# Splitting the output weights early and reloading both parts from DRAM

## The chip, the cores and the metric

One Trainium2 chip, one core of it. The metric is the device time of one execution in microseconds (us). Unchanged programs give times that spread by some tenths of a per cent from run to run.

## The reference

One decoder layer over 1024 tokens of width 1024, in float32:

```python
h      = x @ w_in                      # pool part | q | k | v | forget gate
pool   = pool_mixer(...)               # 512 columns, four groups of 128
attn   = forgetting_attention(...)     # 512 columns, 8 heads of 64, causal
x      = layer_norm(ALPHA * x + concat(pool, attn) @ w_out)
x      = layer_norm(ALPHA * x + square(relu(x @ w_mlp1)) @ w_mlp2)
```

The change concerns `w_out` alone, a matrix of 1024 x 1024 (4 MB): 8 blocks of 128 rows.

## The kernel before

Float32 products are made of three matmuls: each operand `a` is split into a high part `hi` (a cast to the type fp32r, on ScalarE) and the remainder `lo = a - hi` (a subtraction, on VectorE), and `hi*hi + hi*lo + lo*hi` is summed (`split` at L70 to L72, `three` at L81).

The stages follow each other in program order: projection of v and the gate, three of the four pool groups, the attention in four pairs of heads (`order`, L434), the product with `w_out` and the first layer norm, the two products of the MLP and the second norm. Attention goes in units `(p, e, m)`: pair p, head e of the pair, block m of 256 query rows; 8 units a pair. In the first three pairs m falls from 3 to 0, in the last pair it rises, so that the early rows of the mixer are done first. The loop at L437 makes the probabilities of one unit (`att_probs`) and then the values of the unit before (`att_values`). Between these pieces `fillstep` puts matmuls of another job into TensorE's queue, so that it has work while it waits for VectorE and ScalarE: in the first three pairs the q and k projection of the next pair (`qk_proj`, 96 matmuls each), in the last pair the last pool group (`last_fill`: `pool_group(0)`, 48 matmuls, then `pool_linear(0)`).

In `att_probs` GpSimd adds the causal mask to a row of gate sums (L342, first three pairs only), VectorE adds that row to the scores and takes the minimum (L355), ScalarE takes the exponential (L357). In `att_values` TensorE transposes the probabilities (L377), ScalarE casts them (L378), VectorE forms the remainder (L379), TensorE multiplies with v (L393), and ScalarE and VectorE take the result out (L398, L399).

The order of the instructions on each engine and in each queue is fixed when the program is built: a list scheduler walks the program with a priority by program order and takes a later instruction early when its engine and its buffers are free. So the loads and splits of the output weights (L480 to L486), which stand behind the attention in the program, were taken into the last pair of heads. Each engine then executes its own list in order, and an instruction that waits holds up all behind it.

Buffers in SBUF come from classes with a fixed count: `S` (3 of them) holds float32 data on its way to a split, `B` (14) holds split weights, x and v, `Q` (10) and `A` (9) the rest. Every load of weights for a projection (`load_w`, L74) takes an `S` and a `B`. The split output weights take four `B`, two blocks of rows in each.

At L484 SyncE issues the load of one block of `w_out` into an `S`; L485 splits it into its place in `B`. The mixer's output goes through DRAM (`mix_dram`): the attention's at L400, that of the last pool group at L282. It is loaded at L759, split, and multiplied with the output weights at L785.

Of the kernel before, what the change touches and what calls it, by code (L numbers as in the profile page):

```python
# [8 lines left out]
F32 = mybir.dt.float32  # L9
# [3 lines left out]
ALU = mybir.AluOpType  # L13

P = 128
S = 1024
D = 1024
NT = S // P
KT = D // P
# [6 lines left out]
CH = 512  # L26
# [10 lines left out]
def trunk(ctx, tc, xT, xn, wuqk, wvf, bf, poolw, pscale, wout, g1, b1, w1, w2, g2, b2, out):  # L37
# [5 lines left out]
    nc = tc.nc  # L43
    sb = ctx.enter_context(tc.tile_pool(name="sb", bufs=1, reuse_waits="tile"))
    ps = ctx.enter_context(tc.tile_pool(name="ps", bufs=1, space=bass.MemoryType.PSUM))
    dr = ctx.enter_context(tc.tile_pool(name="dr", bufs=1, space=bass.MemoryType.DRAM))
# [4 lines left out]
    def slot(tag, shape, dt=F32R):  # L51
        uid[0] += 1
        return sb.tile([P] + list(shape), dt, tag=tag, bufs=NBUF[tag], name=f"{tag}{uid[0]}")
# [16 lines left out]
    def split(hi, lo, src):  # L70
        nc.scalar.copy(hi, src)  # L71
        nc.vector.tensor_tensor(lo, src, hi.bitcast(F32), ALU.subtract)  # L72
# [34 lines left out]
    ncf_dram = dr.tile([NH, S], F32, name="ncf_dram")  # L107
    rin_dram = dr.tile([NH, S], F32, name="rin_dram")
    mix_dram = dr.tile([4, P, 8, 256], F32, name="mix_dram")


    xs = {}
# [125 lines left out]
    def run(gen):  # L238
        for _ in gen:
            pass  # L240
# [29 lines left out]
    def pool_linear(g, slots):  # L270
        st = slot("S", [P], F32)
        nc.sync.dma_start(st, poolw[:, g])
        pw = slot("U", [2, P])
        split(pw[:, 0], pw[:, 1], st)
        dh, dl = pooled[g]
        mx = slot(slots, [S], F32)
        for c in range(NCH):
            cs = slice(c * CH, (c + 1) * CH)
            dst = bank("mm" if g in LATE else None)
            three(dst, (pw[:, 0], pw[:, 1]), (dh[:, cs], dl[:, cs]), True, True)  # L280
            nc.scalar.activation(mx[:, cs], dst, AF.Copy, scale=ps_sb[:, g : g + 1])
        nc.sync.dma_start(mix_dram[:, :, g, :].rearrange("m p t -> p m t"), mx.rearrange("p (m t) -> p m t", m=4))  # L282
# [39 lines left out]
    def gate_row(h):  # L322
        if h not in gate_rows:
            gate_rows[h] = slot("A", [S], F32)
            rsum[h] = small([P, NT], "rsum", bufs=3)
            nc.sync.dma_start(gate_rows[h], ncf_dram[h : h + 1, :].to_broadcast([P, S]))
# [94 lines left out]
    def last_fill():  # L421
        for g in LATE:
            yield from pool_group(g, "mm")
            pool_linear(g, "Q")
# [3 lines left out]
    def fillstep():  # L428
        fill["credit"] += fill["rate"]
        while fill["credit"] >= 1.0:  # L430
            fill["credit"] -= 1.0
            next(fill["gen"], None)

    order = [(p, e, m) for p in range(NPAIR - 1) for e in range(2) for m in (3, 2, 1, 0)]  # L434
    order += [(NPAIR - 1, e, m) for m in range(4) for e in range(2)]
    pend = None
    for n, unit in enumerate(order):  # L437
        p = n // 8
        if n % 8 == 0:
            if p + 1 < NPAIR:  # L440
                gen, pieces, over = qk_proj(p + 1, "mm"), 4 * KT + 1, 28
            else:
                gen, pieces, over = last_fill(), (2 * KT + 2) * len(LATE), 14
            fill.update(gen=gen, credit=0.0, rate=pieces / over)
        prob = att_probs(*unit)
        if n + 1 < len(order):
            gate_row(2 * order[n + 1][0] + order[n + 1][1])
        if pend is None:
            for g in EARLY[1:]:
                pool_linear(g, "A")  # L450
        fillstep()
        if pend is not None:
            att_values(*pend)
        pend = (*unit, prob)
        if n % 8 == 7:
            run(gen)
    att_values(*pend)
# [22 lines left out]
    for kp in range(KT // 2):  # L480
        hi, lo = slot("B", [2, D]), slot("B", [2, D])
        for k in range(2):
            st = slot("S", [D], F32)
            nc.sync.dma_start(st, wout[2 * kp + k])  # L484
            split(hi[:, k], lo[:, k], st)  # L485
            wo.append((hi[:, k], lo[:, k]))  # L486

    def load_row(tag, src):
# [266 lines left out]
    for m in range(4):  # L755
        mh = []
        for half in range(2):
# [8 lines left out]
            hi, lo = slot("Q", [4, 256]), slot("Q", [4, 256])  # L766
# [389 lines left out]
```

## Time and profile before

| | us |
|---|---|
| median of 3 runs | 1048.75 |
| lowest, highest | 1047.0, 1049.51 |
| the profiled execution | 1046.21 |
| its span, first to last instruction | 1044.4 |
| TensorE busy (PE) | 1017.5 |
| VectorE busy (DVE) | 760.6 |
| ScalarE busy (ACT) | 510.3 |
| GpSimd busy (POOL) | 139.0 |

The profile is of one execution, and all durations below are from it. In its views PE is a matmul, PEld the weight load that runs beside it, SPq the queue in which SyncE issues DMAs. A busy time of PE counts a matmul from its start to a modelled end: two of 512 columns in a row start 0.23 us apart and are counted with 0.39 us each, so short gaps between matmuls are not seen as idle time. Stages by the trace: the work ahead of the attention to about 112 us, the first three pairs to about 266 us, the last pair to about 318 us (its last matmuls run among the first ones of the output product), the output product and the first norm to about 344 us, then the MLP.

### The profile page before, as it was taken

What the parts mean: (1) busy time and instruction counts of PE and PEld (TensorE: products, weight loads), DVE (VectorE), ACT (ScalarE), POOL (GpSimd) and SP (SyncE); (2) the same over time, 40 slices, a digit from 0 to 9 for tenths busy, and PEclk for the clock granted to TensorE, in tenths of its full rate; (3) what the DMA queues carried; (4) which work ended last, traced back from release to release, by engine and by line L of the source; (5) the groups of instructions that cost most, each with busy time, mean ns of one, the idle gap of its engine ahead of it and who ended that gap; (6) DMA issues with size and microseconds to landing.
All of it is one profiled execution on the core that took longest, in us unless ns stands there. A gap on an engine that the chain in (4) does not pass through costs nothing.

```text
span 1044.4 us, 13990 instructions
## 1 busy us (share of the span) xinstructions
PE 1017.5 (97%) x4958; PEld 845.5 (81%) x4958; DVE 760.6 (73%) x1296; ACT 510.3 (49%) x818; POOL 139.0 (13%) x243
## 2 busy tenths in 40 slices
PE   7999999999989999999999999999999999999995
PEld 7988888878767888888888888888788888888884
DVE  4466678777896896989887878788875666565546
ACT  4414566666774331677666766768621221122152
POOL 0000012121100021112112122120100000000057
PEclk9999999999999999999999999999999999999998
DMA  6211311111346632139756667565999888878753
GB/s 223 82 48 62 121 54 50 36 49 53 104 138 192 202 138 105 62 112 357 293 225 266 238 242 280 212 266 189 343 321 305 283 260 282 274 228 275 234 177 120
DMA packets 111798, 195.81 MB, mean 187 GB/s; under 512 B 9256, under 2 KB 77672, under 8 KB 111728
## 3 DMA queue, kind: packets, MB, share of 16 engines
q1 hardware_dynamic: 95600, 136.71, 39.5%
q0 software_dynamic: 15840, 57.68, 14.1%
q8 instruction: 39, 0.64, 0.3%
q10 hardware_dynamic: 288, 0.52, 0.1%
q14 instruction: 31, 0.25, 0.1%
HBM read 127.18 MB, written 67.70 MB: 187 GB/s over the span
## 4 chain that ended last, share of the span: by engine, by line
PE 53%; DVE 3%; DMA 2%; issue 1%; POOL 0%; ACT 0%; POOLq 0%; SPq 0%; DVEq 0%; ACTq 0%
PE s L962 15%; PE s L608 10%; PE pv L962 8%; PE pt L608 7%; PE mm L608 6%; PE pv L608 4%; PE pt L962 2%; PE mm L962 2%; DVE B L72 1%; DMA S<-in_w_dram 1%; DMA A<-hid_dram 1%; DMA hid_dram<-A 0%; POOL A L562 0%; DVE A L731 0%; ACT A L730 0%
## 5 line engine op out<-in xcount | busy, mean ns | idle before, releaser
L71 ACT CAST B<-S 128x1024 fp32r<-128x1024 f32 (+1 forms) x92 | 78.5, 870 | 171.4 <-DMA S<-in_w_dram 58.6
L72 DVE TENSOR_TENSOR B<-S,B 128x1024 fp32r<-128x1024 f32 (+1 forms) x92 | 90.3, 995 | 33.5 <-ACT B L71 33.5
L608 PE MATMUL s<-B,Q 128*128 128x512 f32 x480 | 113.5, 390 | 0.1
L608 PEld LDWEIGHTS s<-B,Q 128*128 128x128 f32 x480 | 90.0, 188 | 19.2 <-ACT B L71 0.5
L962 PE MATMUL s<-B,Q 128*128 128x512 f32 x390 | 94.8, 390 | 0.0
L962 PEld LDWEIGHTS s<-B,Q 128*128 128x128 f32 x390 | 73.2, 188 | 15.5
L71 ACT CAST Q<-S 128x1024 fp32r<-128x1024 f32 x52 | 54.5, 1050 | 60.4 <-PE s L608 17.0
L962 PE MATMUL s<-B,A 128*128 128x512 f32 x333 | 83.1, 394 | 0.9 <-DMA A<-hid_dram 0.9
L733 POOL DMA_DIRECT2D hid_dram<-A x90 | 48.4, 542 | 219.0 <-ACT A L730 174.2
L962 PEld LDWEIGHTS s<-B,A 128*128 128x128 f32 x333 | 62.5, 188 | 15.5 <-DMA A<-hid_dram 1.4
L72 DVE TENSOR_TENSOR Q<-S,Q 128x1024 fp32r<-128x1024 f32 x52 | 63.3, 1218 | 12.1 <-ACT Q L71 12.0
L608 PE MATMUL pt<-B,Q 128*128 128x512 f32 x300 | 71.6, 389 | 0.0
L608 PE MATMUL mm<-B,Q 128*128 128x512 f32 x300 | 71.6, 389 | 0.0
L393 PE MATMUL pv<-A,B 128*128 128x256 f32 x320 | 63.0, 298 | 4.9 <-ACT A L378 2.8
L393 PEld LDWEIGHTS pv<-A,B 128*128 128x128 f32 x320 | 50.4, 190 | 20.2 <-ACT A L378 10.1
L608 PEld LDWEIGHTS pt<-B,Q 128*128 128x128 f32 x300 | 56.3, 188 | 11.7
L608 PEld LDWEIGHTS mm<-B,Q 128*128 128x128 f32 x300 | 56.3, 188 | 11.7
L379 DVE TENSOR_TENSOR A<-pt,A 128x512 fp32r<-128x512 f32 (+1 forms) x80 | 49.0, 634 | 15.7 <-ACT A L378 15.2
L357 ACT ACTIVATE A<-A,nm 128x1024 f32<-128x1024 f32 (+7 forms) x64 | 49.6, 776 | 18.7 <-DVE nm L355 17.5
L731 DVE TENSOR_TENSOR A<-A,A 128x1024 f32<-128x1024 f32 x45 | 53.6, 1220 | 0.5 <-ACT A L730 0.4
L342 POOL TENSOR_TENSOR A<-A,maskb 128x128 f32<-128x128 f32 x48 | 22.4, 467 | 235.9 <-DVE nm L355 136.6
L962 PE MATMUL pv<-B,Q 128*128 128x512 f32 x204 | 50.3, 390 | 0.0
(408 smaller groups left out, 2305.6 us busy)
## 6 DMA issues: line engine op xcount, KB each, us to landing
hid_dram<-A POOLq DMA_DIRECT2D x105, 512.0 KB, 3.9
S<-in_w_dram SPq DMA_DIRECT2D x62, 512.0 KB, 3.5
Q<-hid_dram SPq DMA_DIRECT2D x101, 256.0 KB, 4.6
A<-hid_dram SPq DMA_DIRECT2D x79, 256.0 KB, 5.1
S<-in_wuqk_dram SPq DMA_DIRECT2D x12, 512.0 KB, 3.2
A<-ncf_dram SPq DMA_DIRECT2D x8, 512.0 KB, 3.6
S<-in_wout_dram SPq DMA_DIRECT2D x8, 512.0 KB
S<-mix_dram SPq DMA_DIRECT2D x8, 512.0 KB, 5.1
```

The lines of the kernel that those rows point to most:

```text
L71: nc.scalar.copy(hi, src)
L72: nc.vector.tensor_tensor(lo, src, hi.bitcast(F32), ALU.subtract)
L342: nc.gpsimd.tensor_tensor(nb[:, qs], nb[:, qs], maskb, ALU.add)
L357: nc.scalar.activation(pt[:, :nk], pt[:, :nk], AF.Exp, bias=nm, scale=-1.0, accum_out=rsum[h][:, i : i + 1])
L379: nc.vector.tensor_tensor(tt[:, 1, ev], tp[:, ev], tt[:, 0, ev].bitcast(F32), ALU.subtract)
L393: nc.tensor.matmul(ov, V[j][:, h].rearrange("p s d -> p (s d)"), tt[:, s, a:b], start=(j == 0 and s == 0), stop=(j == 2 * m + 1 and s == 1),)
L608: nc.tensor.matmul(dst, b[x][:, k], A[a][y][:, k], start=first and k == 0 and i == 0, stop=k == H - 1 and i == 2, skip_group_check=not first,)
L731: nc.vector.tensor_tensor(x, x, hi.bitcast(F32), ALU.subtract)
L733: nc.gpsimd.dma_start(hid_dram[self.u, :, i, AT[name] : AT[name] + 2 * CH], part.rearrange("p q n t -> p (q n t)"))
L962: nc.tensor.matmul(dst, h[:, p_], w[q_], start=first and u == self.us[0] and j == 0, stop=u == self.us[-1] and j == 2, skip_group_check=no ...
```

## The change

Each block of `w_out` is loaded, cast and subtracted within the first three pairs of heads, after the values of the units numbered 2, 4, 6, 10, 12, 14, 18 and 20; both parts lie in an `S` buffer, and GpSimd writes them to a new DRAM tensor, 512 KB each. The subtraction is made in two halves of 512 columns. Where the split stood before, SyncE now issues two loads for each block, of the high part and of the remainder, straight into their place in `B`; the cast and the subtraction there are gone.

```diff
+    wo_dram = dr.tile([KT, 2, P, D], F32, name="wo_dram")
...
+    def split_output_weights(k):
+
+        st, hi = slot("S", [D], F32), slot("S", [D])
+        nc.sync.dma_start(st, wout[k])
+        nc.scalar.copy(hi, st)
+        for c in (slice(0, CH), slice(CH, D)):
+            nc.vector.tensor_tensor(st[:, c], st[:, c], hi[:, c].bitcast(F32), ALU.subtract)
+        for i, part in enumerate((hi.bitcast(F32), st)):
+            nc.gpsimd.dma_start(wo_dram[k, i], part)
+
+    SPLIT_AT = {2: 0, 4: 1, 6: 2, 10: 3, 12: 4, 14: 5, 18: 6, 20: 7}
...
         pend = (*unit, prob)
+        if n in SPLIT_AT:
+            split_output_weights(SPLIT_AT[n])
...
         for k in range(2):
-            st = slot("S", [D], F32)
-            nc.sync.dma_start(st, wout[2 * kp + k])
-            split(hi[:, k], lo[:, k], st)
+            for i, part in enumerate((hi, lo)):
+                nc.sync.dma_start(part[:, k].bitcast(F32), wo_dram[2 * kp + k, i])
             wo.append((hi[:, k], lo[:, k]))
```

## Rows read from the trace of the kernel before

**Rows 1.** The page: busy time of each engine, and the shares of the chain that ended last.

```profile
PE 1017.5 (97%) x4958; PEld 845.5 (81%) x4958; DVE 760.6 (73%) x1296; ACT 510.3 (49%) x818; POOL 139.0 (13%) x243
...
PE 53%; DVE 3%; DMA 2%; issue 1%; POOL 0%; ACT 0%; POOLq 0%; SPq 0%; DVEq 0%; ACTq 0%
```

**Rows 2.** Busy time of each engine by stage: the stretch and its length, then PE, PEld, DVE, ACT and POOL with the number of instructions, the granted clock of TensorE as a share of full speed, the busy share of the DMA engines, GB/s.

```profile
112.00:266.00 154.00, 151.43 (x875) 125.06 (x873) 114.88 (x276) 97.48 (x209) 26.81 (x68) 1.00 0.16 51
...
266.00:298.00 32.00, 31.62 (x190) 25.76 (x189) 26.59 (x73) 24.35 (x59) 2.55 (x8) 1.00 0.38 130
298.00:318.00 20.00, 15.16 (x87) 11.99 (x87) 17.56 (x37) 15.21 (x29) 0.62 (x2) 0.91 0.49 160
...
318.00:344.00 26.00, 25.91 (x135) 21.77 (x134) 17.30 (x28) 10.32 (x17) 0.31 (x1) 1.00 0.56 172
```

**Rows 3.** The same view in pieces of 2 us at the end of the last pair.

```profile
300.00:302.00 2.00, 1.43 (x13) 1.14 (x12) 1.91 (x4) 2.00 (x5) 0.00 (x0) 1.00 0.01 4
302.00:304.00 2.00, 1.03 (x10) 0.79 (x8) 2.00 (x4) 1.62 (x3) 0.31 (x1) 1.00 0.00 1
304.00:306.00 2.00, 1.27 (x5) 0.77 (x5) 2.00 (x5) 0.81 (x2) 0.00 (x0) 1.00 0.13 33
306.00:308.00 2.00, 1.53 (x4) 1.24 (x5) 2.00 (x6) 0.36 (x1) 0.00 (x0) 0.66 0.70 244
308.00:310.00 2.00, 2.00 (x7) 1.71 (x7) 1.97 (x4) 1.90 (x4) 0.00 (x0) 0.50 0.09 27
310.00:312.00 2.00, 1.60 (x10) 1.17 (x10) 0.92 (x3) 2.00 (x6) 0.00 (x0) 0.98 1.03 295
...
314.00:316.00 2.00, 0.70 (x7) 0.47 (x6) 1.48 (x7) 1.97 (x5) 0.14 (x1) 1.00 0.67 228
```

**Rows 4.** TensorE's instructions in order of time, 296 to 326 us: start, duration, line, output and inputs, count, and in brackets how long the engine had been idle and what ended that. The last row is the first matmul of the output product.

```profile
301.41 0.51 PE L393 MATMUL pv<-A,B 128*128 128x256 f32 x2 [0.57 <-ACT A L378]
...
304.28 0.73 PE L83 MATMUL mm<-Q,U 128*128 128x512 f32 x2 [1.25 <-ACT Q L71]
...
306.46 0.65 PE L84 MATMUL mm<-Q,U 128*128 128x512 f32 x1 [0.92 <-DVE Q L72]
...
315.88 0.51 PE L393 MATMUL pv<-A,B 128*128 128x256 f32 x2 [1.30 <-ACT A L378]
...
318.44 0.50 PE L83 MATMUL s<-B,Q 128*128 128x512 f32 x1
```

**Rows 5.** VectorE in the same stretch. `B<-S,B` is the subtraction of an output weight block, `Q<-Q,Q` at L72 that of the last pool group.

```profile
297.54 1.22 DVE L72 TENSOR_TENSOR B<-S,B 128x1024 fp32r<-128x1024 f32 x1
...
304.08 1.20 DVE L72 TENSOR_TENSOR B<-S,B 128x1024 fp32r<-128x1024 f32 x1
305.20 1.21 DVE L72 TENSOR_TENSOR Q<-Q,Q 128x1024 fp32r<-128x1024 f32 x1
...
308.75 1.22 DVE L72 TENSOR_TENSOR B<-S,B 128x1024 fp32r<-128x1024 f32 x1
```

**Rows 6.** ScalarE from 284 us on. L251 takes out the first half of the last pool group's projection, `B<-S` is the cast of an output weight block, `Q<-Q` that of the last pool group.

```profile
285.20 0.56 ACT L251 COPY Q<-mm 128x512 f32<-128x512 f32 x1
...
299.92 1.06 ACT L71 CAST B<-S 128x1024 fp32r<-128x1024 f32 x1
...
303.18 1.04 ACT L71 CAST Q<-Q 128x1024 fp32r<-128x1024 f32 x1 [0.18 <-DVE Q L264]
```

**Rows 7.** Groups by line and shape from 266 to 318 us: the eight subtractions and the eight casts of the output weights (count, total busy us, mean ns, idle time of the engine just before them).

```profile
L72 DVE TENSOR_TENSOR B<-S,B 128x1024 fp32r<-128x1024 f32 x8 | 9.7, 1211 | 0.0
...
L71 ACT CAST B<-S 128x1024 fp32r<-128x1024 f32 x8 | 8.4, 1046 | 0.7 <-DMA S<-in_wout_dram 0.7
```

**Rows 8.** GpSimd. The mask adds of 110 to 240 us with shortest, median and longest duration, and who waited for them (us, times); one of them and the VectorE instruction that ran beside it; and, from the MLP, the DMAs that GpSimd issues with 512 KB each: duration of one issue, and time to landing.

```profile
L342 POOL TENSOR_TENSOR A<-A,maskb x38: 425/428/1345, 117.2 to 234.0; 128x128 f32<-128x128 f32 x38
...
  DVE A L355: 2.9, 6
...
175.68 1.34 POOL L342 TENSOR_TENSOR A<-A,maskb 128x128 f32<-128x128 f32 x1 [0.18 <-DVE nm L355]
...
175.52 1.22 DVE L72 TENSOR_TENSOR B<-S,B 128x1024 fp32r<-128x1024 f32 x1
...
L733 POOL DMA_DIRECT2D hid_dram<-A x90: 531/531/767, 464.6 to 739.5; - x90
...
DMA to landing us min/median/max: 2.9/4.0/8.0
```

**Rows 9.** Loads and stores of SyncE's queue: the loads of projection weights (KB, us to landing), one of them and the cast that uses it, the eight loads of output weights (duration of an issue, first and last start), the store of the last pool group's output and the first load of the mixer's output behind it, and how long mask adds had waited for gate rows (us, times).

```profile
S<-in_wuqk_dram SPq DMA_DIRECT2D x3, 512.0 KB, 3.2
...
151.54 0.35 SPq L76 DMA_DIRECT2D S<-in_wuqk_dram  x1
...
167.31 1.03 ACT L71 CAST B<-S 128x1024 fp32r<-128x1024 f32 x1
...
L484 SPq DMA_DIRECT2D S<-in_wout_dram x8: 332/342/348, 224.6 to 297.2; - x8
...
309.15 0.38 SPq L282 DMA_DIRECT2D mix_dram<-Q  x1
...
312.37 0.33 SPq L759 DMA_DIRECT2D S<-mix_dram  x1
...
  DMA A<-ncf_dram: 2.7, 4
```

## The prediction

> **What bounds the kernel now.** I read the page first. TensorE is busy for 97% of the span, and more than half of the chain that ended last is its matmuls [rows 1]. The change adds and removes no matmul, so all it can move is time in which TensorE stands idle or runs slowly. The second view is therefore the busy time by stage [rows 2]: what the reader is to see is the difference between the length of a stretch and PE in it. The first three pairs lose 154.00 - 151.43 = 2.57 us. The last pair loses 0.38 us up to 298 us, and then 20.00 - 15.16 = 4.84 us in its last 20 us, where the granted clock also averages 0.91. The next 26 us lose 0.09. So there is one bad place, and the change takes work out of it.
>
> The third view is that place in pieces of 2 us [rows 3]. VectorE is busy for 1.91 to 2.00 of each 2 us from 300 to 310, while TensorE falls to 1.03. [...] Time lost by the clock: 0.34 x 2 + 0.50 x 2 + 0.02 x 2 = 1.72 us. What the engine did before it fell is in the rows above: it stood idle for 0.57 + 0.97 + 0.73 us in the 6 us ahead. The fourth view, the three engines in order of time, says why [rows 4 to 6]. There is no fill left. TensorE waits 1.25 us for the cast of the last pool group, 0.92 us for its remainder, 0.57 us and later 1.30 us for the cast of transposed probabilities. Among these stand the last casts and subtractions of output weights.
>
> **What the change removes.** Eight subtractions, 9.7 us of VectorE, and eight casts, 8.4 us of ScalarE, all between 266 and 318 us [rows 7]. What each is worth depends on its place:
>
> - The subtraction at 304.08 stands straight ahead of the pool group's remainder at 305.20 [rows 5]. Its input was ready at 303.18 + 1.04 = 304.22 [rows 6], so the remainder can come 1.0 us earlier, and the wait of 0.92 us goes. Value 0.92.
> - The cast at 299.92 delays the next cast, and so TensorE by 0.57 us. But TensorE then reaches the pool group's cast the earlier and waits longer there: 1.25 becomes about 1.8. I count nothing.
> - The wait of 1.25 us is the latency of the pool group's own chain, and that of 1.30 us has only attention work ahead of it. They stay.
> - The clock. With 0.92 us of the idle time gone, the fall may not come. In 314 to 316 us TensorE is busy for only 0.70, and the clock stays up [rows 3]. I take it that the fall goes: 1.72 us.
> - The six splits up to 298 us stand in a stretch that loses 0.38 us in all. I count 0.38 us, as the most they can be worth.
>
> Sum 0.92 + 1.72 + 0.38 = 3.0 us. Lower end 0.9, if the clock falls all the same. Upper end everything but the two waits that stay: 0.38 + 4.84 + 1.72 - 1.25 - 1.30 = 4.4 us.
>
> **What it adds to the first three pairs.** Eight casts of 1.05 us (8.4 us), sixteen half subtractions of 1.21 / 2 = 0.61 us (9.7 us), sixteen GpSimd DMA issues of 0.53 us (8.5 us) [rows 7, 8]. Over the 154 us VectorE goes from 74.6% busy to (114.88 + 9.7) / 154 = 80.9%, ScalarE from 63.3 to 68.8%, GpSimd from 17 to 23% [rows 2]. None becomes the bound. But the engines work in order, so each insertion makes what is behind it later: behind a half subtraction stand the minima of L355 and the remainders of L379, and TensorE waits for both; behind a cast stand L378 and the exponentials. The cover is the fill matmuls and the unit's lead.
>
> How much comes through, from both sides. Lower end: the stretch 266 to 298 us took six splits in 32 us, had fill matmuls as the first pairs have, and lost 0.38 us, so 0.06 us for one, 0.5 us for eight. Upper end: without fill, one cast and one subtraction cost 0.57 and 0.92 us, 0.75 us for each on average, 6.0 us for eight if a split pays that once. The first pairs are nearest to the former: they have fill, and VectorE is 83% busy in those 32 us against 81% here. Because short gaps are not seen in PE's busy time I double the lower end: 0.13 us for each, 1.0 us.
>
> **What moves in the queues.** SyncE's eight loads of output weights move from 225 to 297 us to about 115 to 250 us, past the gate rows, the projection loads and the stores. The DMA engines are 16% busy there, so bandwidth costs nothing. A gate row could come later by the length of a load ahead of it; mask adds already waited for gate rows four times, 2.7 us in all [rows 9]. I take nothing and keep this for the upper end.
>
> The buffers: a split holds two of the three `S`, the longest from its load to the landing of its writes: 3.2 + 1.05 + 1.21 + 2 x 0.53 + 4.0 = 10.5 us [rows 7 to 9]. A projection load needs one. The one shown was issued 15.8 us ahead of its cast and takes 3.2, so it has 12.6 us to spare, more than 10.5. Cost nothing; if two splits come before one load, the cast is up to 21.0 - 12.6 = 8.4 us late, and the fill behind it with it.
>
> In the last pair sixteen loads take the place of eight, and they need `B` directly. Three of the four `B` come free when the first half of the last pool group's projection is done, near 285 us [rows 6]; twelve loads of 0.52 MB are 6.3 MB, at the 295 GB/s of the busiest piece 21 us, so they end near 306 us, ahead of the first use at 318.44. The store at 309.15 and the load at 312.37 stand behind them in the same queue, which makes this the nearest thing to a new wait. Cost nothing; if the loads slip, up to 2 us.
>
> [...] The mask add is between two minima of VectorE: it waits for one and the next waits for it. Its median is 0.43 us, but the one at 175.68 took 1.34 us, and beside it VectorE ran a subtraction of two SBUF inputs from 175.52 to 176.74. So a subtraction stretched a mask add by 0.9 us [rows 8]. [...]
>
> **The sum.** -3.0 + 1.0 = -2.0 us. The profiled execution's 1046.2 us becomes 1044.2. The median of the runs is 2.5 us above the profiled execution, and I shift it by the same amount: 1048.75 - 2.0 = 1046.7 us.
>
> **The rivals.**
>
> 1. *The gain moves on.* The wait that goes is replaced by the next one: TensorE meets the pool group's cast earlier, the clock falls as before, and the first output matmul goes on waiting for store, load and split of the pool group's output (309.15, 312.37, 318.44). For it: two of the four waits are not made by output weights. Against it: the store itself stands behind the removed subtraction. -0.9 + 1.0, about 1048.8 us.
> 2. *GpSimd's queue makes the minima late.* A mask add can stand behind the issue of a write that itself waits for the subtraction, 0.53 us, and be stretched by a half subtraction, 0.61 us. VectorE's next minimum, and with it TensorE, is then up to 1.1 us late for each split. For it: the 1.34 us row; VectorE has waited for mask adds six times already. Against it: those six cost 2.9 us together, and VectorE is idle for 39 us in the stretch. It decides from 3.0 / 8 = 0.38 us for a split: above that the kernel is slower. At 0.8 us: -3.0 + 6.4 = +3.4, 1052.1 us.
> 3. *The whole place closes up.* Without 3.6 us of subtractions VectorE isn't full after 297 us, and all but the two fixed waits go: -4.4 + 0.5 = -3.9, 1044.8 us.
> 4. *It doesn't do what it says:* the scheduler places the loads into `B` so late that the output product waits for them. At 2 us lost this too is about 1048.7 us, and I put it with the first.
>
> **How the numbers follow.** About 0.3%, 3.1 us, is what a measurement of this kernel can tell from no change. Forecast 0.40, first and fourth rival 0.26, second 0.15, third 0.19. Faster by more than 3.1 us means below 1045.6: most of the third and a part of the forecast's own spread (1045.0 to 1048.2), 0.30 together. Slower, above 1051.9: most of the second, 0.14. The rest 0.56. The range leaves out the far ends of the second and third: 1043.5 to 1051.3 us. The likeliest case's own range is 1045.0 to 1048.2.
>
> **What would show it.** Right: in the pieces from 300 to 312 us VectorE below 2.00, the granted clock at 1.00, the wait of 0.92 us gone and the first output matmul 1 to 3 us earlier; in the first three pairs PE's idle time at 3 to 4 us instead of 2.57. The second rival would show as mask adds above 0.43 us and a larger wait of L355 for L342. The first would show as the same waits ahead of the first output matmul, with other names. I am wrong if the scheduler orders the last pool group's chain otherwise, because then the waits that I kept change too.

## The result: the first pairs cost more than the last pair gains

| | before | after |
|---|---|---|
| median, lowest to highest of 20 runs each, us | 1046.38 (1043.6 to 1049.51) | 1050.85 (1047.66 to 1055.65) |
| ratio, 95% interval | | 1.0049 [1.0039, 1.0059] |
| the profiled execution, its span | 1046.21, 1044.4 | 1051.09, 1049.3 |

The change is slower by half a per cent, about 5 us, where 2 us less were forecast. The busy times of TensorE, VectorE and ScalarE hardly differ from [rows 1], as they had to; GpSimd's grow by its writes:

```profile
PE 1018.0 (97%) x4958; PEld 844.7 (81%) x4958; DVE 760.6 (72%) x1304; ACT 510.2 (49%) x818; POOL 149.4 (14%) x259
```

The view that tells is again the busy time by stage (columns as in [rows 2]). In this execution the first pairs begin 3 us sooner than in before and end about 6 us later. The first pairs, then the last pair and the output product:

```profile
112.00:266.00 154.00, 145.79 (x828) 120.33 (x827) 117.28 (x278) 100.80 (x208) 34.38 (x79) 0.98 0.35 119
266.00:298.00 32.00, 30.80 (x181) 23.97 (x180) 22.02 (x64) 17.68 (x49) 3.58 (x10) 1.00 0.51 163
298.00:318.00 20.00, 18.21 (x116) 14.91 (x114) 16.89 (x43) 14.30 (x33) 0.62 (x2) 1.00 0.86 296
318.00:344.00 26.00, 23.81 (x129) 19.34 (x128) 16.59 (x28) 11.12 (x20) 0.62 (x2) 1.00 0.70 212
```

TensorE now loses 154.00 - 145.79 = 8.2 us in the first 154 us, where [rows 2] lost 2.57, and the clock slipped there to 0.98. In pieces of 25 us nearly all of it lies in the first pair. Four pieces of the change, then the first two of before:

```profile
110.00:136.00 26.00, 23.11 (x122) 19.18 (x121) 17.74 (x40) 16.97 (x31) 5.74 (x12) 0.93 0.58 204
136.00:161.00 25.00, 20.60 (x107) 16.68 (x106) 16.22 (x39) 13.31 (x27) 6.30 (x13) 0.93 0.42 144
161.00:186.00 25.00, 24.94 (x144) 20.01 (x144) 22.37 (x55) 17.85 (x38) 6.58 (x14) 1.00 0.47 150
186.00:211.00 25.00, 25.00 (x147) 20.60 (x146) 19.76 (x48) 17.59 (x40) 6.60 (x17) 1.00 0.39 137
...
110.00:136.00 26.00, 25.96 (x141) 21.13 (x140) 18.20 (x43) 15.32 (x30) 3.14 (x8) 1.00 0.22 75
136.00:161.00 25.00, 24.78 (x148) 20.80 (x147) 18.91 (x47) 16.19 (x36) 4.43 (x12) 1.00 0.14 44
```

The first two pieces lose 2.9 + 4.4 us (0.3 in before), the next two 0.1. The splits are not spread as the program places them: the scheduler took them early, so that the eight casts start between 101.97 and 207.03 us, five of them by 157 us, and three fall into the two pieces that lose nothing. The two places in order of time; the first has its cause on ScalarE (SPq is SyncE's issue, x2 two issues with the time between them; L441 loads a block, L442 casts it, L446 writes it out). The last row is from the list of what SyncE's queue waited for (total us, times, longest):

```profile
103.34 0.77 POOL L446 DMA_DIRECT2D wo_dram<-S  x1 [7.17 <-ACT S L442]
...
104.86 0.54 POOL L446 DMA_DIRECT2D wo_dram<-S  x1 [0.75 <-DVE S L444]
...
108.97 12.04 SPq L441 DMA_DIRECT2D S<-in_wout_dram  x2
...
112.56 1.05 ACT L442 CAST S<-S 128x1024 fp32r<-128x1024 f32 x1 [5.28 <-DMA S<-in_wout_dram]
113.63 0.59 ACT L316 ACTIVATE Q<-pt 64x512 fp32r<-64x512 f32 x1
...
116.62 0.45 PE L351 MATMUL s<-Q,Q 128*128 128x384 f32 x1 [2.89 <-DVE nm L357]
...
SPq L441 <- DMA wo_dram<-S: 6.7, 2, 5.1
```

The scheduler put the cast of the second block into ScalarE's list in the first unit, well ahead of its place in the program. It stands there 5.28 us for its load. The load was issued at 108.97, because SyncE waited 5.1 us for the first block's writes to leave their `S` buffer. Behind the cast wait the casts of q (L316), the scores and the minima. So TensorE stands idle (it is busy for 1.73 of the 4 us from 112 to 116), and from 116 to 120 us its clock is down to 0.73. The second place is 30 us later (L402 stores a unit's output, L328 requests the gate row of the next head; the first two rows are the first score matmul and the same request in before, all others are the change's):

```profile
113.57 0.39 PE L349 MATMUL s<-Q,Q 128*128 128x512 f32 x1
...
134.23 0.33 SPq L326 DMA_DIRECT2D A<-ncf_dram  x1
...
110.58 0.39 PE L351 MATMUL s<-Q,Q 128*128 128x512 f32 x1
...
139.90 0.47 SPq L402 DMA_DIRECT2D mix_dram<-U  x1
...
140.42 0.58 SPq L328 DMA_DIRECT2D A<-ncf_dram  x1
...
147.59 0.42 POOL L344 TENSOR_TENSOR A<-A,maskb 128x128 f32<-128x128 f32 x1 [6.85 <-DMA A<-ncf_dram]
147.65 0.69 DVE L357 CUSTOM_DVE_ANT_0 A<-s,A 128x512 f32<-128x512 f32 x1 [3.48 <-DMA A<-ncf_dram]
148.40 0.60 PE L351 MATMUL s<-Q,Q 128*128 128x384 f32 x1 [3.39 <-DVE nm L357]
```

and the stretch around it in pieces of 4 us:

```profile
144.00:148.00 4.00, 1.01 (x6) 0.60 (x5) 0.52 (x2) 1.64 (x3) 0.41 (x2) 1.00 0.92 307
148.00:152.00 4.00, 3.60 (x11) 2.91 (x12) 3.78 (x11) 1.50 (x3) 1.12 (x4) 0.57 0.09 34
```

The gate row's request stands behind a store in SyncE's queue and goes out 29.8 us after the first score matmul, against 20.6 in before; units 0 to 3 come out 5 to 7 us behind before, which is most of these 9 us. The mask add that waits for it starts 7.2 us later (147.59), while the DMA engines are 92% busy with writes of split parts and loads of weights, and TensorE is busy for 1.01 of 4 us. Then the clock falls to 0.57. The row is one line of gate sums for a head, but laid into all 128 partitions it moves as much as the load of a weight block; in before it took 3.6 us to landing:

```profile
A<-ncf_dram SPq DMA_DIRECT2D x8, 512.0 KB, 3.6
...
S<-in_wuqk_dram SPq DMA_DIRECT2D x12, 512.0 KB, 7.4
```

The second row, from the page of the change, shows the same for the loads of projection weights: 7.4 us to landing, 3.2 in before [rows 9].

In the last pair, TensorE in order of time (as [rows 4]; the last row is the first matmul of the output product):

```profile
309.08 0.66 PE L379 MATMUL pt<-ident,A 128*128 128x128 f32 x4 [0.33 <-ACT row L414]
311.65 0.47 PE L351 MATMUL s<-Q,Q 128*128 128x512 f32 x1 [1.21 <-DVE nm L357]
316.91 0.51 PE L395 MATMUL pv<-A,B 128*128 128x256 f32 x2 [0.24 <-ACT A L380]
319.28 0.66 PE L379 MATMUL pt<-ident,A 128*128 128x128 f32 x4 [0.70 <-DVE A L381]
320.67 0.50 PE L395 MATMUL pv<-A,B 128*128 128x256 f32 x2 [0.20 <-ACT A L380]
321.40 0.51 PE L395 MATMUL pv<-A,B 128*128 128x256 f32 x2 [0.22 <-DVE A L381]
325.54 0.50 PE L83 MATMUL s<-B,Q 128*128 128x512 f32 x1 [1.00 <-ACT Q L71]
```

The waits of 1.25, 0.92 and 1.30 us are gone, and so is the fall of the clock. New are 1.21 for minima and 1.00 for the first output product.

### The profile page after: what moved, and what is told of

It reads as the page before. It is cut to its first block, busy times and chain, and to the rows that moved or that the text cites. A ratio compares the mean times of both kernels' runs of the same rounds, so it can differ in the third digit from the quotient of the medians.

```text
span 1049.3 us, 14086 instructions
## 1 busy us (share of the span) xinstructions
PE 1018.0 (97%) x4958; PEld 844.7 (81%) x4958; DVE 760.6 (72%) x1304; ACT 510.2 (49%) x818; POOL 149.4 (14%) x259
## 4 chain that ended last, share of the span: by engine, by line
PE 53%; DMA 2%; DVE 2%; POOL 1%; ACT 0%; issue 0%; POOLq 0%; DVEq 0%; SPq 0%; ACTq 0%
PE s L976 16%; PE s L622 9%; PE pv L976 8%; PE pt L622 6%; PE mm L622 6%; PE pv L622 4%; PE pt L976 2%; PE mm L976 2%; DMA S<-in_w_dram 1%; DMA hid_dram<-A 1%; DMA A<-hid_dram 1%; DVE A L745 0%; DVE B L72 0%; DVE Q L72 0%; POOL A L576 0%
## 5 line engine op out<-in xcount | busy, mean ns | idle before, releaser
L71 ACT CAST B<-S 128x1024 fp32r<-128x1024 f32 (+1 forms) x84 | 70.2, 853 | 171.7 <-DMA S<-in_w_dram 60.5
L72 DVE TENSOR_TENSOR B<-S,B 128x1024 fp32r<-128x1024 f32 (+1 forms) x84 | 80.7, 973 | 35.7 <-ACT B L71 35.7
L622 PEld LDWEIGHTS s<-B,Q 128*128 128x128 f32 x480 | 90.0, 188 | 19.2 <-ACT B L71 0.6
L976 PEld LDWEIGHTS s<-B,Q 128*128 128x128 f32 x390 | 73.2, 188 | 15.6
L71 ACT CAST Q<-S 128x1024 fp32r<-128x1024 f32 x52 | 54.6, 1051 | 62.2 <-PE s L622 17.2
L747 POOL DMA_DIRECT2D hid_dram<-A x90 | 48.2, 539 | 218.6 <-ACT A L744 174.1
L72 DVE TENSOR_TENSOR Q<-S,Q 128x1024 fp32r<-128x1024 f32 x52 | 63.3, 1216 | 14.4 <-ACT Q L71 14.2
L381 DVE TENSOR_TENSOR A<-pt,A 128x512 fp32r<-128x512 f32 (+1 forms) x80 | 49.2, 633 | 16.2 <-ACT A L380 15.7
```

The lines of the kernel that those rows point to most:

```text
L381: nc.vector.tensor_tensor(tt[:, 1, ev], tp[:, ev], tt[:, 0, ev].bitcast(F32), ALU.subtract)
L622: nc.tensor.matmul(dst, b[x][:, k], A[a][y][:, k], start=first and k == 0 and i == 0, stop=k == H - 1 and i == 2, skip_group_check=not first,)
L747: nc.gpsimd.dma_start(hid_dram[self.u, :, i, AT[name] : AT[name] + 2 * CH], part.rearrange("p q n t -> p (q n t)"))
L976: nc.tensor.matmul(dst, h[:, p_], w[q_], start=first and u == self.us[0] and j == 0, stop=u == self.us[-1] and j == 2, skip_group_check=no ...
```

## Markers for all kernels

Times in us from the first score matmul of the same execution (it lies at 110 to 118 us of the span, differing from execution to execution): the start of VectorE's instruction that takes out the output of units 0, 4 and 23 (L399 in before), then the first MLP matmul, then this less unit 23, which is the last pair with the output product. Each row is one profiled execution, and some lie off the median of their kernel: e2 by 3.3, e3 by 4.4 and e11 by 2.1 us below it, e8 by 4.4 above.

| | unit 0 | unit 4 | unit 23 | MLP | MLP - 23 |
|---|---|---|---|---|---|
| before | 15.5 | 41.0 | 165.3 | 304.0 | 138.7 |
| the change | 20.7 | 54.6 | 174.1 | 311.5 | 137.4 |
| e1_lastpair | 15.6 | 41.1 | 164.6 | 302.5 | 137.9 |
| e2_nowrite | 16.4 | 42.4 | 166.4 | 304.2 | 137.8 |
| e3_firstpairs | 19.2 | 51.3 | 171.7 | 309.3 | 137.6 |
| e4_late | 16.3 | 43.7 | 167.2 | 304.3 | 137.1 |
| e5_xwrites | 23.4 | 49.2 | 173.5 | 312.6 | 139.1 |
| e6_behind | 15.5 | 45.1 | 168.6 | 306.1 | 137.5 |
| e7_half | 17.1 | 42.8 | 167.5 | 304.8 | 137.3 |
| e8_late9 | 16.3 | 43.3 | 167.3 | 308.5 | 141.2 |
| e9_gpsub | 15.5 | 41.1 | 169.9 | 313.9 | 144.0 |
| e10_latebehind | 15.6 | 41.2 | 165.9 | 304.2 | 138.3 |
| e11_behind2 | 15.5 | 46.9 | 175.4 | 312.4 | 137.0 |
| e12_rows | 19.4 | 44.3 | 168.2 | 305.1 | 136.9 |
| e13_behindrows | 15.5 | 41.9 | 164.5 | 301.9 | 137.4 |
| e14_lbrows | 15.5 | 41.1 | 164.0 | 300.9 | 136.9 |
| e15_beforerows | 15.6 | 41.1 | 164.9 | 306.6 | 141.7 |

The change falls 5.2 us behind by unit 0 and 13.6 by unit 4, and is 8.8 behind when the first pairs end (9.6 at unit 22: unit 23's output already comes out within the last pair). At the MLP it is 7.5 behind. The two executions as a whole differ by 4.9 only, because the first score matmul of the change lies 3.0 us sooner (110.6 against 113.6 us); whether the change has a part in that is not shown.

## The experiments

The theory formed from the traces: the cost is not the engines' added work but two waits in the first pair, for a load and for a gate row, and both come from the DMA traffic of the splits and from the buffers that it holds. Its rivals: the work on VectorE and ScalarE itself, GpSimd's queue (the second rival of the prediction), and a cost that lies in the last pair. Each of these kernels was run 6 or 12 times, and each ratio is against runs of before that were taken with it; their medians go from 1045.65 to 1047.14 us, so compare ratios and not the medians of different kernels.

**Each half alone.** The last pair as changed, with `wo_dram` filled from x in the v projection and no early split:

```diff
+    for k in range(KT):
+        for i in range(2):
+            nc.gpsimd.dma_start(wo_dram[k, i], xs[1, k].bitcast(F32).rearrange("p a n -> p (a n)"))
...
-        if n in SPLIT_AT:
-            split_output_weights(SPLIT_AT[n])
```

> The last pair alone: no early splits; sixteen loads of prepared parts straight into B, as in the change, where the eight loads, casts and subtractions stood. To have something to load, the DRAM tensor is filled from the x buffers during the projection of v (so the output weights are not the reference's in this kernel). Both theories of the loss (waits for the split's loads, or the added engine work) put the loss into the first pairs, so this kernel should show the gain alone: 2 to 3 us below the kernel before, about 1044 us. If the gain only moves on (first rival of the prediction): within 1 us of before, and the first output matmul as long after the first score matmul as before, 204.8 us.

This kernel leaves the output weights out and multiplies with x's data in their place. Measured 1047.13, 1.0013 [1.0000, 1.0025]. With the filling ahead of it the first score matmul is late (117.5 us, 113.6 in before), so the whole time is no measure of the last pair. From the first score matmul on it is 1.5 us ahead of before at the MLP, and the first pairs are as before.

Then the opposite, the early splits and writes, and the last pair as before:

```diff
-            for i, part in enumerate((hi, lo)):
-                nc.sync.dma_start(part[:, k].bitcast(F32), wo_dram[2 * kp + k, i])
+            st = slot("S", [D], F32)
+            nc.sync.dma_start(st, wout[2 * kp + k])
+            split(hi[:, k], lo[:, k], st)
```

> The first pairs alone: loads, casts, subtractions and writes as in the change, and the last pair splits the original weights again as before. Both theories: the whole loss without the gain. By the trace of the change the outputs of the units ran 9.7 us behind those of before at the end of the first pairs, so 7 to 10 us above before, about 1055 us; ScalarE waits for a split's load by over 4 us once.

Measured 1055.32, 1.0099 [1.0080, 1.0119]. The whole loss is here, and more: in the last pair the predicted waits stand as they were, 1.25 and 0.93 us for the pool group, then 1.41 and 1.29:

```profile
309.09 0.72 PE L83 MATMUL mm<-Q,U 128*128 128x512 f32 x2 [1.25 <-ACT Q L71]
...
311.28 0.50 PE L84 MATMUL mm<-Q,U 128*128 128x512 f32 x1 [0.93 <-DVE Q L72]
```

So taking the splits out of the last pair does remove these waits.

**The work without the writes.** Last pair as before, eight early loads, casts and subtractions, and no write:

```diff
-        for i, part in enumerate((hi.bitcast(F32), st)):
-            nc.gpsimd.dma_start(wo_dram[k, i], part)
```

> The engine work alone: loads, casts and half subtractions in the first three pairs as in the change, but no write to DRAM, so an S buffer is free again at the subtraction; the last pair splits as before. Wait theory (the load of a split waits until the writes of the split before have landed, and ScalarE stands in its queue until that load has landed): no wait of ScalarE above 2 us for a load in the first pair, and 0 to 3 us above before, about 1048 us. Work theory (28 us of added instructions make everything behind them late): the cost stays, 8 to 10 us above before, about 1055 us.

Measured 1047.32, 1.0017 [1.0006, 1.0028]. With all the added work of VectorE and ScalarE the first pairs end 1.1 us behind before in the profiled execution. The load of the second block goes out 3.6 us sooner, and the cast waits 1.62 instead of 5.28:

```profile
105.33 7.07 SPq L441 DMA_DIRECT2D S<-in_wout_dram  x2
...
109.61 1.05 ACT L442 CAST S<-S 128x1024 fp32r<-128x1024 f32 x1 [1.62 <-DMA S<-in_wout_dram]
```

That left open whether the writes hurt by holding `S` or by their traffic. So the same writes, behind the subtraction, but out of x's buffers; `S` is free once the parts are formed (last pair as before):

```diff
+    power2 = small([P, 1], "power2")
...
-        for i, part in enumerate((hi.bitcast(F32), st)):
-            nc.gpsimd.dma_start(wo_dram[k, i], part)
+        seen = nc.gpsimd.tensor_copy(power2, st[:, 0:1])
+        with tc.issue_after(seen.ins):
+            for i in range(2):
+                nc.gpsimd.dma_start(wo_dram[k, i], xs[1, k].bitcast(F32).rearrange("p a n -> p (a n)"))
```

> As the run of the first pairs alone (9.5 us above before), but GpSimd's sixteen writes take their data from a buffer of x and not from the two S buffers of the split; they stay behind the subtraction in GpSimd's queue, so number, size and about the place of the writes are kept, and the S buffers are free at the subtraction (what is written is not the output weights, and nothing reads it). Buffer theory (the loads wait for the landing of writes that hold S): the cost falls to that of the run without writes, 1 to 3 us above before, 1047 to 1049 us. Traffic theory (the writes' 8 MB in the DMA queues and GpSimd's issue time make gate rows and loads late): the cost stays, 7 to 10 us above before, 1053 to 1056 us.

Measured 1052.12, 1.0061 [1.0042, 1.0079]. My theory of the buffer alone fell here: the load goes out early, and its cast waits 3.77 us all the same. Both writes of the first block are under way beside it (issued from 105.30 us), and from 108 to 112 us the DMA engines are 87% busy, against 19% in the run without writes:

```profile
105.46 9.25 SPq L442 DMA_DIRECT2D S<-in_wout_dram  x2
...
111.81 1.05 ACT L443 CAST S<-S 128x1024 fp32r<-128x1024 f32 x1 [3.77 <-DMA S<-in_wout_dram]
119.20 1.05 ACT L443 CAST S<-S 128x1024 fp32r<-128x1024 f32 x1 [3.01 <-DMA S<-in_wout_dram]
```

**Other places.** The splits after the units 8, 10, 12, 14, 16, 18, 20 and 22:

```diff
-    SPLIT_AT = {2: 0, 4: 1, 6: 2, 10: 3, 12: 4, 14: 5, 18: 6, 20: 7}
+    SPLIT_AT = {8: 0, 10: 1, 12: 2, 14: 3, 16: 4, 18: 5, 20: 6, 22: 7}
```

> The change with its eight splits after units 8, 10, 12, 14, 16, 18, 20, 22, so none belongs to the first pair of heads. The work is the same. Wait theory: the two stalls came where two splits in a row and the projection loads of the first pair wanted the same three buffers; the five splits in the second and third pair cost nothing in the trace of the change, so the time is that of before less the gain: 1043 to 1046 us. Work theory: the same 8 to 10 us are lost, later: 1050 to 1053 us.

Measured 1046.12, 1.0002 [0.9991, 1.0013]; 1.9 us behind at the end of the first pairs, and the gain that was expected on top does not show. Late splits with the last pool group's fill over 9 steps instead of 14 (`over = 9`):

> The change with late splits (after units 8 to 22, equal to before within 0.3 us) and the last pool group's matmuls spread over 9 fill steps instead of 14. If the gain of the last pair is lost because the first output matmul waits for the pool group's chain of store, load and cast, that chain starts some 10 us earlier here and the gain comes out: 1 to 3 us below before, 1043 to 1045 us. If the end of the last pair is bound by the attention's own chain, fill matmuls that are gone too early leave TensorE idle: 0 to 3 us above before.

Measured 1047.00, 1.0016 [1.0004, 1.0027]. A miss: 0.14%, about 1.5 us, above the late splits. In the profiled execution, which lies 4.4 us above the median of its twelve, the last pair takes 141.2 us instead of 137.1, TensorE waits up to 1.61 us, and the clock falls to 0.82 and 0.76 at 328 to 336 us. This fits a fill that is used up too early, but no run tests it further. Sixteen half blocks, each with both parts in one `S`:

```diff
+            w = slot("S", [2, CH])
+            hi, st = w[:, 0], w[:, 1].bitcast(F32)
+            nc.sync.dma_start(st, wout[k][:, c])
+            nc.scalar.copy(hi, st)
+            nc.vector.tensor_tensor(st, st, hi.bitcast(F32), ALU.subtract)
+            nc.gpsimd.dma_start(wo_dram[k].rearrange("i p n -> p i n")[:, :, c], w.bitcast(F32))
```

> The change with sixteen half splits: half a block and its high part share one S buffer, each half block is loaded (256 KB), cast, subtracted and written (512 KB, one DMA) by itself. Same bytes, eight loads more, the same number of writes; a split holds one of three S at a time instead of two. Buffer theory: the load of the next half finds a free S, ScalarE's longest wait for a split's load falls from 5.3 to under 2 us, total 1045 to 1048 us. Traffic theory: as the change, 1050 us or more.

Measured 1046.33, 1.0011 [1.0000, 1.0023], with 2.2 us lost in the first pairs; the longest wait of a cast for its load is 3.9 us, not under 2 as expected.

**The first wait removed.** The change, and each cast stands behind the last exponential of its own unit in ScalarE's list:

```diff
+    exps = []
...
-            nc.scalar.activation(pt[:, :nk], pt[:, :nk], AF.Exp, bias=nm, scale=-1.0, accum_out=rsum[h][:, i : i + 1])
+            exps.append(nc.scalar.activation(pt[:, :nk], pt[:, :nk], AF.Exp, bias=nm, scale=-1.0, accum_out=rsum[h][:, i : i + 1]))
...
-        nc.scalar.copy(hi, st)
+        with tc.issue_after(exps[-1].ins):
+            nc.scalar.copy(hi, st)
```

> The change with one edge more: the cast of each split stands behind the last exponential of its own unit in ScalarE's list, so the scheduler cannot take it into an earlier gap. Loads, writes and buffers are as in the change. Wait theory (ScalarE stands at a cast whose load has not landed, and all behind it is late): the stall ahead of the first unit goes, and units run at most 3 us behind before at the end of the first pairs instead of 8.8; total 1045 to 1047 us. Work theory and traffic theory: nothing changes, 1050 to 1051 us.

Measured 1046.79, 1.0004 [0.9993, 1.0014]. No cast of a split waits for its load any more, and unit 0 is as in before. The edge also moves the splits: the first cast starts at 131.64 us instead of 101.97, so this run does not tell the cast's wait from early traffic. At unit 4 it is 4.1 us behind, and GpSimd waits 5.64 us for the gate row. Next, the edge for blocks 0 and 1 alone (`if k < 2`):

> The change, with the cast of blocks 0 and 1 alone behind the last exponential of their unit; the other six stay where the change has them. If the first pair's two stalls are all of the cost, the same as with the edge for all eight, about 4 us below the change and within 1 us of before. If the later six have a part in it, between the two.

Measured 1053.88, 1.0066 [1.0045, 1.0088], no better than the change: a miss that showed a third form of the same wait. With the later casts free to be placed early, splits hold the `S` buffers, two casts wait 3.4 us for a write to leave one, and the casts of projection weights, which feed the fill, wait for loads issued too late:

```profile
173.17 1.04 ACT L71 CAST B<-S 128x1024 fp32r<-128x1024 f32 x1 [4.29 <-DMA S<-in_wuqk_dram]
...
200.97 1.04 ACT L71 CAST B<-S 128x1024 fp32r<-128x1024 f32 x1 [4.76 <-DMA S<-in_wuqk_dram]
```

**The second wait removed.** The change, and the gate row of the next head requested one unit earlier:

```diff
             gate_row(2 * order[n + 1][0] + order[n + 1][1])
+        if n + 2 < len(order) and p < NPAIR - 1:
+            gate_row(2 * order[n + 2][0] + order[n + 2][1])
```

> The change, with one edit: the gate row of the next head is requested one unit earlier in the first three pairs. The second stall (minima waiting 3.48 and mask adds 6.85 us for a gate row that lands late) should go, the first (a cast that waits 5.28 us for its load) stay. If the gate row decides the second stall, 3 to 5 us below the change, about 1 us above before; if the split's cast decides it and the gate row only follows, 0 to 1.5 us below the change.

Measured 1048.22, 1.0017 [1.0004, 1.0030]. The gate row goes out 18.6 us after the first score matmul, and no minimum waits for it; unit 4 comes from 13.6 to 3.3 us behind. So the two waits are not independent: either repair takes some 10 us of unit 4's lag. The first wait stays, as it should:

```profile
110.55 12.03 SPq L441 DMA_DIRECT2D S<-in_wout_dram  x2
...
114.13 1.05 ACT L442 CAST S<-S 128x1024 fp32r<-128x1024 f32 x1 [5.24 <-DMA S<-in_wout_dram]
```

**Both removed, and the control.** The change with both edits, the edge for all eight:

> The change with both repairs: every cast of the early splits behind the last exponential of its own unit, and the gate row of the next head requested one unit earlier. The edge alone left the first output of unit 4 about 4 us behind the kernel before, with GpSimd waiting 5.6 us for a gate row; early gate rows alone left 3 us behind, with the cast waiting 5.24 us for its load. If these two waits are the cost, the first pairs end at most 1 us behind before, and what is left of the gain shows: 0 to 1.5 us below the kernel before. If something third costs, 2 us or more above it.

Measured 1043.36, 0.9965 [0.9952, 0.9977], faster than both kernels. The first pairs end level with before, with all eight splits and all sixteen writes in them: 0.1 us behind at unit 22, and 0.8 us ahead at unit 23, as in the run with the last pair alone:

```profile
112.00:266.00 154.00, 151.78 (x875) 124.88 (x875) 125.03 (x295) 104.15 (x218) 38.88 (x85) 1.00 0.41 137
266.00:298.00 32.00, 31.89 (x195) 25.86 (x195) 21.49 (x67) 20.36 (x56) 2.56 (x8) 1.00 0.73 245
298.00:318.00 20.00, 16.85 (x104) 13.18 (x103) 16.73 (x38) 14.51 (x29) 0.93 (x3) 1.00 0.67 222
318.00:344.00 26.00, 25.65 (x127) 21.04 (x126) 17.90 (x26) 8.05 (x11) 0.00 (x0) 1.00 0.75 212
```

VectorE and ScalarE are busier there than in the change (125.03 against 117.28 us, 104.15 against 100.80), because none of the splits now lies ahead of the stretch and the units come sooner, and TensorE loses 2.22 us, less than in [rows 2]. The first matmul of the output product waits 0.15 us.

Late splits with the edge, and then with both edits:

> Late splits (after the units 8, 10, ... 22) and, in addition, each cast behind the last exponential of its own unit in ScalarE's list. If the late splits still lose something to a cast that stands early, 0.5 to 1 us below the run of late splits, that is up to 1 us below the kernel before. If late splits cost nothing in the first pairs and what is missing of the gain is the last pair's own, the same as the late splits, 1.0000 to 1.0005 of before.

Measured 1045.28, 0.9990 [0.9976, 1.0004].

> Late splits (after the units 8, 10, ... 22), the edge and the early gate rows together, as the most that this placing can give. Late splits with the edge stand at 0.999 of before with 0.6 us lost in the first pairs. If the gate rows still cost something there, 1 us lower; if the 0.6 us is VectorE's and ScalarE's own added work, the same 0.999.

Measured 1043.58, 0.9972 [0.9960, 0.9983]. With both repairs early and late splits are the same within their intervals. And early gate rows on the kernel before, without the change:

> The kernel before, with one edit: the gate row of the next head is requested one unit earlier in the first three pairs. It is the control for the run in which this edit took 2.6 us off the change. If early gate rows help only beside the change's traffic, the same as before, within 0.5 us. If they help by themselves (mask adds waited 2.7 us for gate rows in before), up to 2 us below before, and then that run's gain is no measure of what the change did to the gate rows.

Measured 1046.0, 0.9990 [0.9978, 1.0001]. So early rows by themselves bring 0.1%, about 1 us (by the interval nothing to 0.2%), and the rest of 0.9965 is the change's with its repairs.

**The relief alone.** The kernel before, with the subtraction of the last pair on GpSimd:

```diff
-            split(hi[:, k], lo[:, k], st)
+            nc.scalar.copy(hi[:, k], st)
+            nc.gpsimd.tensor_tensor(lo[:, k], st, hi[:, k].bitcast(F32), ALU.subtract)
```

> The kernel before, with one edit: in the last pair the remainder of the output weights is formed on GpSimd instead of VectorE. Nothing goes through DRAM and nothing is split early, so this is the relief of VectorE at the end of the last pair by itself, without sixteen loads and without any cost in the first pairs. If the predicted terms hold (0.92 of the wait for the pool group's remainder, 1.72 of the clock), the time is 2 to 3 us below the kernel before. If the gain moves on to the next waits, as it did in the run with the last pair alone (about 1 us), the time is 0 to 1.5 us below. If subtractions of 1024 columns on GpSimd stretch VectorE's instructions or come too late for the output product, 1 to 3 us above.

Measured 1055.7, 1.0083 [1.0064, 1.0102], a miss by far. Two subtractions of 2.4 us on GpSimd, and beside them two casts on VectorE, 2.24 and 3.05 us, that take 0.42 us at the median in before; TensorE waits for the minima behind them, and this is half of the loss (4.6 us at unit 23). The last row is a later place: an instruction of a single column, in the pool group's chain, takes 2.30 us (0.15 in before) beside a GpSimd subtraction that started at 308.16, and behind it the clock falls to 0.50 (312 to 316 us):

```profile
272.94 4.85 POOL L486 TENSOR_TENSOR B<-S,B 128x1024 fp32r<-128x1024 f32 x2 [6.12 <-ACT Q L314]
273.35 2.24 DVE L317 CAST Q<-Q 64x512 fp32r<-64x512 f32 x1
...
275.52 3.05 DVE L318 CAST Q<-Q 64x512 fp32r<-64x512 f32 x1
...
278.96 0.58 PE L349 MATMUL s<-Q,Q 128*128 128x256 f32 x1 [4.74 <-DVE nm L355]
...
308.53 2.30 DVE L263 TENSOR_TENSOR Q<-Q,icnt 128x1 f32<-128x1 f32 x1
```

## Why the prediction was wrong, point by point

**The step that failed** is "What moves in the queues" in the first pairs. Three terms were set to nothing. Bandwidth, because the DMA engines were 16% busy: that is a mean, and where the splits' loads and writes meet, the share is 0.92, and from a gate row's request to the mask add that waits for it 7.2 us pass. The gate rows, "I take nothing and keep this for the upper end": 3.48 us of waiting for VectorE, and with the clock's fall to 0.57 behind it most of the second loss. The `S` buffers, "Cost nothing": I compared the time that a split holds them with the spare time of a projection load, and not with the next split's own load, whose cast the scheduler had taken early; it waited 5.28 us. And I had the loads spread over 115 to 250 us, where the casts came between 102 and 207, five of them by 157. The bound that I gave for projection loads, up to 8.4 us, shows in one experiment as 4.29 and 4.76.

Their size by the measured ratios: the change against the change with both repairs is 1.0049 - 0.9965 = 0.84%, 8.8 us; without the 0.1% that early gate rows may bring by themselves, 7.7 us. By the trace the change is 8.8 us behind at the end of the first pairs. I had 1.0 for all of it. My sign for being right, 3 to 4 us without TensorE work in the first pairs, reads 8.2 us, and the first output matmul comes 10.1 us later after the first score matmul than in before (215.0 against 204.9) and not 1 to 3 sooner; with both repairs it comes 0.85 sooner.

That 1050.85 still lies inside 1043.5 to 1051.3 us is luck: these were counted from 1048.75, the median of three runs, which twenty runs put at 1046.38.

**The added work** of VectorE and ScalarE, at 0.13 us for a split, 1.0 in all, was not too low. Without writes it costs 1.1 us by the trace and 0.17%, 1.8 us, by the measured ratio [1.0006, 1.0028], part of it the wait of 1.62; with both repairs nothing can be seen of it.

**The gain of 3.0 us** is of the right order. The run with both repairs stands 0.9990 - 0.9965 = 0.25%, 2.6 us, below the control (each of the two is known to 0.12%). The change stands 1.0099 - 1.0049 = 0.50%, 5.2 us, below the first pairs alone, which had six runs and the wider interval. By the traces it is less: the last column of the markers has a mean of 139.0 us for the five kernels with the splits as before in the last pair (before, e2, e3, e5, e15) and of 137.4 for the ten without them (e8 with its other fill and e9 left out), 1.6 us; counted from unit 22, so that what unit 23 gains is in it, 144.4 and 142.1, 2.3 us. How much it is stays open, since one execution's last pair differs from another's by more (137.6 to 141.7 among those five). By its terms: the wait of 0.92 us went, as predicted. The waits of 1.25 and 1.30 us, which I had kept ("They stay"), went too, and 1.21, 0.70 and 1.00 took their place. The fall of the clock went, but it is no sure price: of the five with the splits in the last pair it shows in before and in the control (0.82 and 0.75 at 316 to 324 us) and not in the other three.

**The rivals.** The first, the gain moves on, happened in part: the first output matmul waits 1.00 us, and the store of the pool group's output is followed by its load after 4.0 us (315.39 to 319.39; 3.2 in [rows 9]), with the DMA engines 0.73 to 1.02 busy in the pieces of 4 us around it. Against the run with both repairs (3.5 us and 0.15 us of wait) this is 0.5 and 0.85 us. The second named the right sign and about the size (+3.4 us) for the wrong cause: minima did come late, by the gate row's landing and not by GpSimd's queue, and three waits of VectorE for mask adds come to 1.3 us in all (2.9 in [rows 8]). The third, the whole place closes up, did not happen. The fourth is excluded: the last load into `B` is issued at 311.50, the product starts at 325.54 and waits for a cast.

**GpSimd beside VectorE.** In the change, mask adds go up to 1.35 us, as in before. Beside half subtractions two of them took 0.80 and 0.96 us (130.48, 138.87; the median is 0.43), so these two were stretched beside them, but with 1.3 us of waiting in all it decides nothing. The other way round it is dear: in the run with GpSimd's subtractions VectorE's first cast, 2.24 us, ends at 275.59, just behind the first of the two subtractions (272.94 + 4.85 / 2 = 275.37). Why the two casts took longer there was not shown. Not every VectorE instruction was held up: beside the subtraction at 287.05 to 289.46 us minima took 0.56 and 0.67 us and a unit's output 0.41, as elsewhere.

Still open: how the first wait divides between the buffer held by a write and the shared DMA engines. Without writes 3.66 us of it go, with the buffer free but the traffic kept 1.51; both matter, but in the latter run other loads moved as well. The whole times say the same: with the last pair as before, 1.0099 as changed, 1.0061 with the buffers free, 1.0017 without writes. That a load slows beside GpSimd's writes is read from the run with the buffers free, where the cast waited 3.77 us; how the DMA engines divide their time between the queues was not shown.

## What to carry to other kernels

Work that is moved into a stretch with a spare engine still brings its loads and writes: look for what is queued behind each of them in that stretch, and at the DMA share there (0.92 where the gate row came late), not at the mean (0.35 over the first three pairs). A cast that a scheduler takes early becomes a wait of its whole engine if its load can be late (5.28 us here); an edge that keeps it behind the current unit's work, and a request for urgent data (a gate row) ahead of the bulk, turned a loss of half a per cent into a gain of a third of one, of which the early request alone may have brought 0.1%. Repair one wait at a time and then all: each alone left a time near before's, and only both together showed what the change was worth.

## What the runs showed of the hardware that I had not expected

- A gate row that is broadcast to 128 partitions, 512 KB in all, has landed 7.2 us after its issue, by the start of the mask add that waited for it, beside 512 KB writes and loads (DMA share 0.92), against 3.6 at the median in before; loads of projection weights, 512 KB each, take 7.4 us at the median against 3.2.
- After TensorE stood idle for 3 of 4 us (144 to 148 us in the change) the granted clock averaged 0.57 in the next 4.
- A subtraction of 128x1024 from SBUF takes 2.4 us on GpSimd and 1.21 on VectorE, and beside it casts of 64x512 on VectorE take 2.24 and 3.05 us instead of 0.42 at the median; two instructions that take in scores, of 384 and 512 columns, took 0.56 and 0.67 us beside one, against 0.56 and 0.69 in before.
